# Layer two of a hybrid decoder trunk: half of K of both u blocks by seven products beside the V blocks

## The chip, the core and the metric

The kernel runs on one core of a Trainium2 chip. A core has a matrix engine (TensorE, PE in the profile, with its weight loads as PEld), a vector engine (VectorE, DVE), a scalar engine (ScalarE, ACT), a general one (GpSimd, POOL) and a queue that only issues transfers (SyncE, SP). Each engine works through its own instructions in order and waits on semaphores for the others. The metric is the device time of one execution in microseconds (us), lower is better.

## The reference

Two layers over x of 256 tokens by 2048 features, all in float32. What matters here is the first half of a layer:

```python
h = rms_norm(x, norm1_g[l])
z = h @ w_in[l]                       # columns: u 1024 | v 1024 | q 1024 | k 256 | v_attn 256
z_sgu = gelu(z[..., :2048])
u, v = split(z_sgu, 2)                # v: rms_norm per head of 64, then a causal 128x128 mix per head
out_a = u * (einsum('hts,bcshd->bcthd', tril(w_s), v) + b_s)
out_b = swa_sink_attention(q, k, v_attn)   # q and k normed per head, 16 query heads, window 128
mixed = concat(rms_norm(out_a), rms_norm(out_b))
x = x + mixed @ w_out[l]
x = x + (silu(h2 @ w_gate) * (h2 @ w_up)) @ w_down    # h2 = rms_norm(x, norm2_g), 5632 wide
```

## The kernel before

**A product in float32 from three matmuls.** Activations stand transposed in SBUF, 128 features by 256 tokens, as a pair of a high and a low part. Weights come as tiles of 128x1024 float32, two K-tiles of 512 columns (512 KB, `raw`, eight buffers). `split2` makes two tiles of each: ACT casts `wh` (five buffers), DVE subtracts for the rest `wl` (four buffers). `mm3` then issues high by high, high by low, low by high. A `unit` is one weight tile for both token halves, twelve matmuls of 128x512. PE, DVE and ACT thus go through the same list of weight tiles, DVE and ACT ahead by at most the buffers.

**Seven products.** A 2x2 block product (Strassen's scheme in Winograd's form) needs seven block products in place of eight. `seven` does it in five PSUM banks, `seven_low` in three. A step of these uses one weight tile for six matmuls (one combination of tokens), so each weight tile, split at the same cost, feeds half as many matmuls as in a unit. Sums of weight tiles are made by DVE (`raw` plus `ys`, `ss`) and by DMAs that accumulate, issued by POOL. The activations need sums as well, `ext`, which `combine` makes of the normed x. In both layers seven products serve q, gate and up (ten blocks of eleven), and half of K of two column blocks of `w_out`.

**The order of layer two's first half.** The code is emitted in the order of a clock (`tick`) that counts units. What hangs on a result is put off by so many units with `later` (numbers in tables such as `Q_T`, `SPATIAL_AT`, `U_AT`), and a scheduler then orders each engine's instructions. While the last down product of layer one runs, q of layer two goes beside it, thirty steps spread over `Q_UNITS` units by `q_to`. Blocks follow: k with v_attn, V0, V1, u0, u1, eight units each. The norms per head (`head_inv`) take squares on ACT, sums on DVE, a power on POOL (`inv_rms`, L210), and then a scaling on DVE (`scaled`, L583 for q in two pairs of halves, L732 for V). The six pieces of attention (`attend`) and the spatial mixes are strewn between the units of V1, u0 and u1. `u_gated` ends a u block. Then `PARTS` orders the units of `w_out` with the steps of its `seven_low` (`s`).

**PSUM.** Eight banks: five in `pa` (`acc`, `m`, `l`), two in `pd` (`dacc`), one in `pm`. Small tiles (scores, transposes) take turns in all three, or in `pm` alone while `solo` is set.

Of the kernel before, what the change touches and what calls it, by code (L numbers as in the profile page):

```python
# [12 lines left out]
F32 = mybir.dt.float32  # L13
# [36 lines left out]
UNIT_AT = ((7.5, 10, 12.5, 15.5, 18, 20.5), (8, 11, 14, 17, 21, 25))  # L50
KV_NORM = (31, 0)
KV_T = (8, 6)
# [8 lines left out]
Q_T = (((4, 6), (6, 9)), ((4, 6), (4, 7)))  # L61
SPATIAL_AT = (((8, 10), (9, 11)), ((6, 9), (7, 10)))
U_AT = (((5, 8), (2, 4)), ((3, 7), (2, 3)))
END_AT = (((21, 23.5), (25.9, 27)), ((22, 27), (31, 33)))
S_OUT = (True, True)
# [7 lines left out]
    "a0 a0 s a0 s a0 a1 a1 s a1 s a1 s b0 s b0 s b0 s b0 s b1 s b1 s b1 s b1 s s b2 b2 b2 b2 b3 b3 b3 b3",  # L73
# [14 lines left out]
def trunk(ctx, tc, x, xt, w_in, w_q, w_out, w_oa, w_gate, w_up, w_down, sgu_w, sgu_g, consts,  # L88
# [22 lines left out]

    def split2(raw):
        wh = wp.tile([P, 2, NB], F32R, tag="wh", name="wh", bufs=5)
        wl = wp.tile([P, 2, NB], F32R, tag="wl", name="wl", bufs=4)
        step = 2 if clock[0] > 1 else 1
        for j in range(0, 2, step):
            src = raw[:, j : j + step, :]
            nc.scalar.copy(wh[:, j : j + step, :], src)  # L118
            nc.vector.tensor_tensor(  # L119
                wl[:, j : j + step, :], src, f(wh[:, j : j + step, :]), ALU.subtract  # L120
            )
        return wh, wl
# [81 lines left out]
    anchor = [None]  # L204

# [91 lines left out]
    def combine(ps, lay, col, ext):  # L297
# [4 lines left out]
        extend(g, ap, "big", ext)  # L302
        return pair
# [96 lines left out]
    def seven_low(src, pairs, ext, out):  # L400
# [19 lines left out]
        def held(name):  # L420
            return tp.tile([P, 2, NB], F32, tag="hT", name=name)
# [3 lines left out]
        for i in range(2):  # L425
            x.append(raw_load(src(0, 0, i)))
            y.append(held("ys"))
            nc.sync.dma_start(y[i], src(0, 1, i))
            b22 = raw_load(src(1, 1, i))
            s.append(held("ss"))  # L430
            half(x[i], acc0, a_op(0, 0), i, True, True)
            yield
            nc.vector.tensor_tensor(x[i], x[i], y[i], ALU.add)
            nc.vector.tensor_tensor(s[i], x[i], b22, ALU.add)
            anchor[0] = nc.gpsimd.dma_start(y[i], src(1, 1, i), accum_op=ALU.add)
        acc1 = bank("l1")
# [15 lines left out]
        out(0, 0, acc0, 1)  # L452
# [3 lines left out]
        nc.vector.tensor_tensor(mp[:, 1], acc1, mp[:, 1], ALU.add)  # L456
        for i in range(2):
            half(s[i], acc2, a_op(1, 1), i, False, True)
            yield
            if i == 0:  # L460
                out(1, 1, mp[:, 1], -1)
        nc.vector.tensor_tensor(mp[:, 0], acc2, mp[:, 0], ALU.add)
        for i in range(2):
            half(raw_load(src(1, 1, i)), acc1, e_op(3), i, False, True)
            yield
            if i == 0:
                out(0, 1, mp[:, 0], 1)
        out(1, 0, acc1, -1)
# [42 lines left out]
    for lay in range(L):  # L511
# [62 lines left out]
        def q_norm(b, lay=lay, layer=layer, qT=qT, qz=qz):  # L574
# [10 lines left out]
            head_inv(qn, 8, scaled)  # L585
# [121 lines left out]
        def v_gate(b, acc, lay=lay, layer=layer, gate=gate, wms=wms):  # L707
# [69 lines left out]
        def norm_block(n, ss, pairs, lay, col, ext=None):  # L777
            def to_T(c):
                lo = n * NB + 2 * c * P
                ps = pm.tile([P, 2, SEQ], F32, tag="sm", name="ps_n")  # L780
                transpose_pair([xres[:, t, lo : lo + 2 * P] for t in range(NTOK)], ps)
                at = col + 4 * n + 2 * c
                pairs.append(
                    split_gain(ps, lay, at, "hT") if ext is None else combine(ps, lay, at, ext)
                )
# [22 lines left out]
        v_gate(0, run(block(2, *beside), with_q))  # L808
        if lay == 0:
            v_gate(1, run(block(3, *beside), with_q))  # L810
        if lay == 0:
# [5 lines left out]
        later(Q1_AT, lambda q_norm=q_norm: q_norm(1))  # L817
# [59 lines left out]
        def complete(n, whole=whole, ss2=ss2, pairs2=pairs2, ext2=ext2, norm_block=norm_block):  # L877
# [3 lines left out]

        low = seven_low(
            lambda r, c, i: w_oa[lay, c, i, r], pairs_a, ext_a,
            lambda c, t, acc, sign: residual(2 + c, t, acc, sign),
# [128 lines left out]
        def down(blocks, lay=lay, pairs_f=pairs_f, norm_block=norm_block, ss1=ss1, pairs1=pairs1, ext1=ext1, left=left, live=live, release=release, accs=accs, full=full, seed=seed, flush=flush, turn_over=turn_over):  # L1013
# [4 lines left out]
            def out_of(n, t, acc):  # L1018
# [12 lines left out]
                if t == NTOK - 1 and final and lay < L - 1:  # L1031
                    norm_block(n, ss1, pairs1, lay + 1, C_G1, ext1)
# [60 lines left out]
        for went in other:  # L1093
# [4 lines left out]
            if lay < L - 1 and done > 0:  # L1098
                q_to(now_q, done / Q_UNITS[1])

# [89 lines left out]
```

## Time and profile before

| | us |
|---|---|
| median of 3 runs (1913.45 to 1914.74) | 1914.46 |
| profiled execution, its time | 1913.7 |
| profiled execution, span from first to last instruction | 1912.0 |
| PE busy | 1903.6 |
| DVE busy | 1725.1 |
| ACT busy | 1361.0 |
| POOL busy | 183.4 |
| layer two, V1 to u1, in the span | about 1056 to 1133 |

PE's busy time is one of overlapping instructions, with modelled ends; the pace of matmuls is read from their starts in the timeline. "Idle before" gives how long an engine stood before an instruction and which instruction released it. Times in the span count from the first instruction.

### The profile page before, as it was taken

How to read it: one execution, taken by the hardware profiler on the slowest of the kernel's cores; microseconds unless marked ns; L12 is line 12 of the kernel's file. 1: busy time of each engine (PE TensorE's matmuls, PEld its weight loads, DVE VectorE, ACT ScalarE, POOL GpSimd, SP SyncE). 2: the span in 40 equal slices, each digit the busy share in tenths (PEclk: the TensorE clock that was granted, in tenths of full speed). 3: DMA queues.
4: the chain of work that ended last, by engine and by line, in shares of the span. 5: the costliest groups of instructions: out<-in, count | busy, mean ns of one | idle time of the engine just before them, and what ended most of it. 6: DMA issues, size and time to landing. Idle time of an engine off the chain costs nothing.

```text
span 1912.0 us, 25453 instructions
## 1 busy us (share of the span) xinstructions
PE 1903.6 (100%) x8764; PEld 1565.2 (82%) x8764; DVE 1725.1 (90%) x1879; ACT 1361.0 (71%) x1829; POOL 183.4 (10%) x180
## 2 busy tenths in 40 slices
PE   9999999999999999999999999999999999999999
PEld 7888888888888888888888888888888888888887
DVE  7988889999999999999797778899999999999993
ACT  8668676677767776777777576766867677776773
POOL 0230001000000001000012200000000100010000
PEclk9999999999999999999999999999999999999999
DMA  9874668878977897888577537697789788888783
GB/s 356 257 288 135 192 201 245 245 244 270 284 231 244 273 289 224 258 254 277 187 230 249 192 118 224 195 277 225 241 273 296 226 255 264 270 245 253 250 276 109
DMA packets 128289, 459.98 MB, mean 241 GB/s; under 512 B 14240, under 2 KB 14624, under 8 KB 128160
## 3 DMA queue, kind: packets, MB, share of 16 engines
q1 hardware_dynamic: 105552, 377.49, 53.7%
q0 software_dynamic: 21888, 79.70, 23.0%
q8 instruction: 68, 1.11, 0.2%
q10 hardware_dynamic: 720, 1.18, 0.2%
q14 instruction: 61, 0.50, 0.1%
HBM read 456.21 MB, written 2.10 MB: 240 GB/s over the span
## 4 chain that ended last, share of the span: by engine, by line
PE 95%; ACT 2%; issue 1%; DVE 1%; DMA 1%; POOL 0%; SPq 0%; DVEq 0%; ACTq 0%; POOLq 0%
PE m L155 15%; PE m L154 15%; PE m L156 15%; PE dacc L154 11%; PE dacc L155 11%; PE dacc L156 11%; PE acc L154 4%; PE acc L155 4%; PE acc L156 4%; PE ps_f L227 1%; PE ps_v L666 1%; PE l L154 1%; PE l L155 1%; PE l L156 1%; PE ps_n L227 1%
## 5 line engine op out<-in xcount | busy, mean ns | idle before, releaser
L118 ACT CAST wh<-raw 128x1024 fp32r<-128x1024 f32 (+1 forms) x794 | 814.7, 1050 | 384.5 <-DVE raw L350 168.3
L119 DVE TENSOR_TENSOR wl<-raw,wh 128x1024 fp32r<-128x1024 f32 (+1 forms) x794 | 945.1, 1219 | 92.4 <-ACT wh L118 26.5
L154 PE MATMUL m<-wh,ext 128*128 128x512 f32 x704 | 276.7, 393 | 0.0
L155 PE MATMUL m<-wl,ext 128*128 128x512 f32 x704 | 274.9, 391 | 0.0
L156 PE MATMUL m<-wh,ext 128*128 128x512 f32 x704 | 274.4, 390 | 0.0
L155 PE MATMUL dacc<-wl,aT 128*128 128x512 f32 x624 | 243.4, 390 | 0.0
L154 PE MATMUL dacc<-wh,aT 128*128 128x512 f32 x624 | 243.2, 391 | 0.0
L156 PE MATMUL dacc<-wh,aT 128*128 128x512 f32 x624 | 243.0, 389 | 0.0
L119 DVE TENSOR_TENSOR wl<-t,wh 128x1024 fp32r<-128x1024 f32 x176 | 213.6, 1223 | 12.9 <-issue 5.4
L118 ACT CAST wh<-t 128x1024 fp32r<-128x1024 f32 x176 | 184.4, 1051 | 37.3 <-DVE t L351 13.6
L154 PE MATMUL m<-wh,hT 128*128 128x512 f32 x528 | 206.4, 391 | 0.0
L155 PE MATMUL m<-wl,hT 128*128 128x512 f32 x528 | 205.7, 390 | 0.0
L156 PE MATMUL m<-wh,hT 128*128 128x512 f32 x528 | 205.5, 389 | 0.0
L155 PEld LDWEIGHTS m<-wl,ext 128*128 128x128 f32 x704 | 132.3, 188 | 28.9 <-DVE wl L119 2.0
L154 PEld LDWEIGHTS m<-wh,ext 128*128 128x128 f32 x704 | 132.2, 188 | 27.5 <-ACT wh L118 0.9
L156 PEld LDWEIGHTS m<-wh,ext 128*128 128x128 f32 x704 | 132.2, 188 | 27.4
L154 PEld LDWEIGHTS dacc<-wh,aT 128*128 128x128 f32 x624 | 117.1, 188 | 25.1 <-ACT wh L118 0.7
L155 PEld LDWEIGHTS dacc<-wl,aT 128*128 128x128 f32 x624 | 117.2, 188 | 24.8 <-DVE wl L119 0.6
L156 PEld LDWEIGHTS dacc<-wh,aT 128*128 128x128 f32 x624 | 117.2, 188 | 24.3
L359 POOL DMA_DIRECT2D t<-in_w_gate_dram x80 | 69.1, 864 | 525.9 <-DVE wl L119 389.7
L156 PEld LDWEIGHTS m<-wh,hT 128*128 128x128 f32 x528 | 99.1, 188 | 20.7
L155 PEld LDWEIGHTS m<-wl,hT 128*128 128x128 f32 x528 | 99.2, 188 | 20.3
(190 smaller groups left out, 2905.7 us busy)
## 6 DMA issues: line engine op xcount, KB each, us to landing
raw<-in_w_gate_dram SPq DMA_DIRECT2D x176, 512.0 KB, 6.1
raw<-in_w_up_dram SPq DMA_DIRECT2D x176, 512.0 KB, 6.0
raw<-in_w_down_dram SPq DMA_DIRECT2D x176, 512.0 KB, 6.0
t<-in_w_gate_dram POOLq DMA_DIRECT2D x80, 512.0 KB, 7.4
raw<-in_w_in_dram SPq DMA_DIRECT2D x76, 512.0 KB, 6.0
raw<-in_w_out_dram SPq DMA_DIRECT2D x48, 512.0 KB, 4.3
raw<-in_w_up_dram POOLq DMA_DIRECT2D x40, 512.0 KB, 6.1
raw<-in_w_q_dram SPq DMA_DIRECT2D x32, 512.0 KB, 4.9
```

The lines of the kernel that those rows point to most:

```text
L118: nc.scalar.copy(wh[:, j : j + step, :], src)
L119: nc.vector.tensor_tensor(wl[:, j : j + step, :], src, f(wh[:, j : j + step, :]), ALU.subtract)
L154: nc.tensor.matmul(acc, ah, wh, start=first, stop=False, skip_group_check=again)
L155: nc.tensor.matmul(acc, ah, wl, start=False, stop=False, skip_group_check=again)
L156: nc.tensor.matmul(acc, al, wh, start=False, stop=last, skip_group_check=again)
L227: nc.tensor.transpose(ps[:, j, t * P : (t + 1) * P], blocks[t][:, j * P : (j + 1) * P], ident)
L359: anchor[0] = nc.gpsimd.dma_start(t2, src(1, 0, i), accum_op=ALU.add)
L666: nc.tensor.matmul(pv[:, r, i], pt[:, (r * n + i) * (t + 1) + b, :], zkv[b][:, cols], start=b == 0, stop=b == t,)
```

## The change

Layer two's u blocks (1024 columns) are no longer sixteen units of `block(0)` and `block(1)`. For the first 1024 rows of K, `seven_low` makes the 2x2 block product (two column blocks by two token halves) in fourteen steps of six matmuls, beside eight units of V1 and the last four of V0; `U_ORDER` gives the order (`v` a unit of V, `s` a step), and the last four steps stand alone. Three results stand in the three banks of the scheme, the fourth (`c22`) in a bank of its own. Then eight units of the other half of K add to these four banks, and `u_gated` follows for both blocks. The scheme's sums of tokens are those that q of layer two already has (`ext1`), kept longer, so those of the first four pairs move to other buffers (`aT`). The weights come a second time in another arrangement (`w_uh`), made on the host.

V1 accumulates in `pa`, V0 in `pd` as before; after V0 the steps and V1 hold all five banks of `pa`.

Query: the thirty steps of q in layer two spread over 20 units in place of 24, with a power of 1.1 on their share. The scalings of q and of V in layer two are emitted with `issue_after` the last `wl`, and later by other gaps (`Q_GAP`, `V_GAP`). The tables for layer two are set anew. In `seven_low` the first sums of weights are emitted before the step's yield, and results go to four functions in `done`.

```diff
-Q_PACE = (1.5, 1)
-GAP = (4.5, 2.5)
+Q_PACE = (1.5, 1.1)
+GAP = (4.5, 4)
+V_GAP = ((4.5, 4.5), (6, 4))
...
-Q_UNITS = (20, 24)
-Q1_AT = 6
+Q_UNITS = (20, 20)
+Q1_AT = (6, 6)
+Q_GAP = (1.5, 2)
...
+U_ORDER = "v s v v s v v s v s v s v s v s v s v s v s"
...
-            nc.vector.tensor_tensor(
+            last_wl[0] = nc.vector.tensor_tensor(
                 wl[:, j : j + step, :], src, f(wh[:, j : j + step, :]), ALU.subtract
             )
...
+    def in_turn(then):
+        def held(r):
+            with tc.issue_after(last_wl[0].ins):
+                then(r)
+
+        return held
...
-    def seven_low(src, pairs, ext, out):
+    def seven_low(src, pairs, ext, done, tag="hT"):
...
-        out(0, 0, acc0, 1)
+        done[0, 0](acc0, None)
...
-        nc.vector.tensor_tensor(mp[:, 1], acc1, mp[:, 1], ALU.add)
+        done[1, 1](acc1, mp[:, 1])
...
-        nc.vector.tensor_tensor(mp[:, 0], acc2, mp[:, 0], ALU.add)
+        done[0, 1](acc2, mp[:, 0])
...
-        out(1, 0, acc1, -1)
+        done[1, 0](acc1, None)
...
-            head_inv(qn, 8, scaled)
+            head_inv(qn, 8, in_turn(scaled) if lay else scaled, Q_GAP[lay])
...
-                head_inv([v[:, t] for t in range(NTOK)], 8, scaled, GAP[lay])
+                head_inv([v[:, t] for t in range(NTOK)], 8, in_turn(scaled) if lay else scaled, V_GAP[lay][b])
...
         if lay > 0:
-            v_gate(1, run(block(3)))
-        for b in range(2):
-            u_gated(b, run(acc_u if lay == 0 and b == 0 else block(b)))
+            us = {}
+
+            def opposite(acc, z, us=us):
+                us[1, 1] = pa.tile([P, NB], F32, tag="acc", name="c22")
+                nc.vector.scalar_tensor_tensor(us[1, 1], acc, -1.0, z, ALU.mult, ALU.subtract)
+
+            def added(acc, z, us=us):
+                us[0, 1] = acc
+                nc.vector.tensor_tensor(acc, acc, z, ALU.add)
+
+            def turned(acc, z, us=us):
+                us[1, 0] = acc
+                nc.scalar.activation(acc, acc, AF.Copy, scale=-1.0)
+
+            low = seven_low(
+                lambda r, c, i: w_uh[0, c, i, r], pairs1, ext1,
+                {
+                    (0, 0): lambda acc, z, us=us: us.update({(0, 0): acc}),
+                    (1, 1): opposite, (0, 1): added, (1, 0): turned,
+                },
+                "aT",
+            )
...
+            v01 = itertools.chain(v_block(0, v0), v_block(1, block(3)))
+            n_v = 0
+            for name in U_ORDER.split():
+                if name == "s":
+                    next(low)
+                    continue
+                n_v += 1
+                next(v01, None)
+                solo[0] = n_v < 25 - Q_UNITS[1]
+                if n_v == 32 - Q_UNITS[1]:
+                    next(v01, None)
+            few[0] = False
+            for _ in range(4):
+                next(low)
+            next(low, None)
+            for b in range(2):
+                acc = [us[b, t] for t in range(NTOK)]
+                for c in range(4, 8):
+                    unit(
+                        w_in[lay, b, c], [(pairs1[c], 0), (pairs1[c], 1)], acc,
+                        False, c == 7, True,
+                    )
+                u_gated(b, acc)
...
-                q_to(now_q, done / Q_UNITS[1])
+                q_to(now_q, (done / Q_UNITS[1]) ** Q_PACE[1])
```

The engines' orders agree between the two kernels up to the end of layer one's last down product. Three places where they differ follow. The names: `wl` is the low part of a weight tile, `hT` and `ext` those of the normed x and its sums, `raw` and `t2` weight tiles and their sums, `ir` a norm's power, `wm` the spatial weights.

DVE, where q's steps go beside the last units of layer one's down product and k's first (the unit of `dacc` whose split is `wl_8952`, later `wl_8951`), before:

```order
L119 TENSOR_TENSOR wl_8952<-raw_8949,wh_8951 128x1024
L119 TENSOR_TENSOR wl_8975<-raw_8967,wh_8974 128x1024
L292 TENSOR_TENSOR ext_8906<-e_8869,ext_8906 128x512
L350 TENSOR_TENSOR raw_8967<-raw_8967,raw_8969 128x1024
L351 TENSOR_TENSOR t2_8973<-raw_8967,raw_8971 128x1024
L119 TENSOR_TENSOR wl_8987<-raw_8967,wh_8986 128x1024
L119 TENSOR_TENSOR wl_8999<-raw_8996,wh_8998 128x1024
L357 TENSOR_TENSOR raw_8969<-raw_8969,raw_8971 128x1024
L119 TENSOR_TENSOR wl_9016<-t2_8973,wh_9015 128x1024
```

And after:

```order
L124 TENSOR_TENSOR wl_8951<-raw_8948,wh_8950 128x1024
L313 TENSOR_TENSOR hT_8878<-g_8875,hT_8878 128x512
L294 SCALAR_TENSOR_TENSOR e_8881<-e_8881,g_8875 128x128
L304 TENSOR_TENSOR ext_8885<-e_8847,ext_8885 128x512
L297 SCALAR_TENSOR_TENSOR e_8881<-e_8881,g_8875 128x128
L362 TENSOR_TENSOR raw_8931<-raw_8931,raw_8933 128x1024
L304 TENSOR_TENSOR ext_8916<-e_8881,ext_8916 128x512
L363 TENSOR_TENSOR t2_8937<-raw_8931,raw_8935 128x1024
L124 TENSOR_TENSOR wl_8969<-raw_8931,wh_8968 128x1024
L369 TENSOR_TENSOR raw_8933<-raw_8933,raw_8935 128x1024
L124 TENSOR_TENSOR wl_8980<-t2_8937,wh_8979 128x1024
```

Before, four splits stood behind the first, three of steps and one of a unit; now there are two, both of steps, and the sums of x's last pair and of the weights stand in one piece ahead of them.

POOL from V0's spatial weights to the last norm of q and V, before:

```order
L695 DMA wm_9215<-in_sgu_w_dram 128x1024
L700 AFFINE_SELECT wm_9215<-wm_9215 128x1024
L604 DMA bias_9364<-in_band_dram 128x1024
L604 DMA bias_9366<-in_band_dram 128x1024
L210 TENSOR_TENSOR ir16_9394<-ms16_9392,mhalf_99 128x16
L210 TENSOR_TENSOR ir16_9423<-ms16_9421,mhalf_99 128x16
L695 DMA wm_9443<-in_sgu_w_dram 128x1024
L700 AFFINE_SELECT wm_9443<-wm_9443 128x1024
L210 TENSOR_TENSOR ir16_9554<-ms16_9552,mhalf_99 128x16
```

And after:

```order
L446 DMA ys_9306<-in_w_uh_dram 128x1024
L222 TENSOR_TENSOR ir16_9353<-ms16_9351,mhalf_99 128x16
L708 AFFINE_SELECT wm_9242<-wm_9242 128x1024
L446 DMA ys_9376<-in_w_uh_dram 128x1024
L452 DMA ss_9310<-in_w_uh_dram 128x1024
L452 DMA ss_9380<-in_w_uh_dram 128x1024
L222 TENSOR_TENSOR ir16_9460<-ms16_9458,mhalf_99 128x16
L703 DMA wm_9535<-in_sgu_w_dram 128x1024
L222 TENSOR_TENSOR ir16_9498<-ms16_9496,mhalf_99 128x16
```

The four accumulating DMAs of the u weights now stand in POOL's queue between the powers; `ir16_9460` is V0's and `ir16_9498` that of q's second pair.

ACT at the end of a u block's transposes, where the first units of `w_out` need `aT`, before (u0's second half, `ps_t_10177`):

```order
L309 ACTIVATE ge_10182<-ps_t_10177,cst_82 128x256 x2
L313 CAST aT_10185<-ge_10182 128x512
L753 ACT_TABLE_LOAD
L753 ACTIVATE u_10225<-acc0_9902,ir2_8791 128x512
L291 CAST ext_10209<-ge_10182 128x512
```

And after (u0's second half, `ps_t_10286`):

```order
L229 ACTIVATE aT_10274<-ps_t_10269,cst_82 128x256
L761 ACT_TABLE_LOAD
L761 ACTIVATE u_10300<-l1_9462,ir2_8808 128x512
L229 ACTIVATE aT_10274<-ps_t_10269,cst_82 128x256
L321 ACTIVATE ge_10291<-ps_t_10286,cst_82 128x256 x2
L761 ACTIVATE u_10302<-c22_9867,ir2_8808 128x512
L325 CAST aT_10294<-ge_10291 128x512
```

The table load and the two gelus of u1 have moved from behind the cast of u0's second half to ahead of it. On PE, that half's transposes stand before one unit and eight transposes ahead of the unit that reads it now (`w_10345`); before, two units, eight transposes and a piece's scores stood between (`w_10271`).

More of the change, by code (lines that the diff above doesn't have):

```diff
@@ L110, in raw_load @@
         return raw
+    last_wl = [None]
     def split2(raw):
@@ L420, in held @@
         def held(name):
-            return tp.tile([P, 2, NB], F32, tag="hT", name=name)
+            return tp.tile([P, 2, NB], F32, tag=tag, name=name)
         x, y, s = [], [], []
@@ L807, in trunk @@
         later(GATE_LOAD[lay][1], lambda gate_load=gate_load: gate_load(1))
-        v_gate(0, run(block(2, *beside), with_q))
         if lay == 0:
+            v_gate(0, run(block(2, *beside), with_q))
             v_gate(1, run(block(3, *beside), with_q))
+        else:
+            v0 = block(2, *beside)
+            for _ in range(Q_UNITS[1] - 16):
+                next(v0)
+                with_q()
         if lay == 0:
```

51 lines of the change are left out of this document (32 added, 19 removed).

## The prediction

> **What bounds the kernel.** First the page: its span, its busy times and the chain that ended last.
>
> ```profile
> span 1912.0 us, 25453 instructions
> ...
> PE 1903.6 (100%) x8764; PEld 1565.2 (82%) x8764; DVE 1725.1 (90%) x1879; ACT 1361.0 (71%) x1829; POOL 183.4 (10%) x180
> ...
> PE 95%; ACT 2%; issue 1%; DVE 1%; DMA 1%; POOL 0%; SPq 0%; DVEq 0%; ACTq 0%; POOLq 0%
> ```
>
> The chain is PE's. Next the waits, for PE over the whole span:
>
> ```profile
> PE heat L193 <- DVE mhalf L195: 1.5, 1, 1.5
> PE acc L154 <- ACT wh L118: 1.1, 1, 1.1
> PE ps_t L227 <- DVE s L622: 0.7, 1, 0.7
> PE acc L155 <- DVE wl L119: 0.2, 1, 0.2
> ```
>
> Four waits, 3.5 us. The kernel gets shorter only by fewer matmuls, or by small losses that are no whole waits. Their pace is read from PE's timeline in V1, the change's place (start, duration, then the instruction):
>
> ```profile
> 1056.05 0.48 PE L154 MATMUL acc<-wh,hT 128*128 128x512 f32 x1
> 1056.50 0.50 PE L155 MATMUL acc<-wl,hT 128*128 128x512 f32 x1
> 1056.84 0.40 PE L156 MATMUL acc<-wh,hT 128*128 128x512 f32 x1
> ...
> 1059.13 1.05 PE L718 MATMUL ps_g<-v,wm 128*128 128x128 f32 x8
> 1059.94 0.48 PE L154 MATMUL acc<-wh,hT 128*128 128x512 f32 x1
> ...
> 1060.71 0.39 PE L154 MATMUL acc<-wh,hT 128*128 128x512 f32 x1
> ...
> 1062.53 0.39 PE L156 MATMUL acc<-wh,hT 128*128 128x512 f32 x1
> 1062.76 0.27 PE L227 MATMUL ps_t<-ident,m 128*128 128x128 f32 x1
> ...
> 1063.11 0.48 PE L154 MATMUL acc<-wh,hT 128*128 128x512 f32 x1
> ...
> 1066.06 1.16 PE L617 MATMUL ps_s<-kT,qT 64*128 64x128 f32 x16
> 1067.15 0.50 PE L154 MATMUL acc<-wh,hT 128*128 128x512 f32 x1
> ```
>
> From 1060.71 to 1062.53 lie eight steps: 0.2275 us a matmul, 2.73 us a unit, 1.37 us a step of six. Four transposes take 0.35 (1062.76 to 1063.11), a spatial half 0.81 (from 1059.13), a piece's scores 1.09 (from 1066.06). At 1056 two matmuls took 0.45 and 0.34 us in place of 0.23 each: 0.33 us lost.
>
> What the others have left is in the windows. The columns after the window are its length, the busy time with the instructions of PE, PEld, DVE, ACT and POOL, then clock, DMA share and GB/s:
>
> ```profile
> 960.00:990.00 30.00, 30.00 (x140) 24.78 (x139) 29.31 (x43) 22.59 (x36) 5.61 (x3) 1.00 0.82 247
> ...
> 1050.00:1080.00 30.00, 29.89 (x159) 23.98 (x157) 23.65 (x37) 17.20 (x34) 12.45 (x5) 1.00 0.51 167
> 1080.00:1110.00 30.00, 30.00 (x179) 25.43 (x180) 23.21 (x38) 21.17 (x47) 1.12 (x2) 1.00 0.52 175
> 1110.00:1140.00 30.00, 30.00 (x168) 24.72 (x168) 21.09 (x37) 21.76 (x49) 0.00 (x0) 1.00 0.32 106
> ```
>
> From 1050 to 1140 DVE idles 22.1 us and ACT 29.9 us. From 960 to 990, where q begins, DVE idles 0.7 us.
>
> **The change part by part.** *Matmuls.* Eight units of twelve, 96 matmuls, become fourteen steps of six, 84. Twelve go, at 0.2275: -2.73 us. The Trainium skill, in TensorE: Matmul & The Clock Gate, section "Back-to-back issue gap", gives 131 ns as the sustained spacing at 512 columns. By it twelve would be worth 1.57 us and the sum below -0.60 (1913.9); this trace has 227.5 ns in all eight steps, so the rule gets no chance here.
>
> *DVE, ACT and transfers in bulk.* Prices from their timelines:
>
> ```profile
> 1049.85 0.69 DVE L732 TENSOR_TENSOR v<-v,ir 128x512 f32<-128x512 f32 x1 [1.64 <-POOL ir L210]
> ...
> 1054.02 0.69 DVE L583 TENSOR_TENSOR m<-m,ir 128x512 f32<-128x512 f32 x1 [1.58 <-POOL ir L210]
> 1054.63 0.69 DVE L583 TENSOR_TENSOR c<-c,ir 128x512 f32<-128x512 f32 x1
> 1055.23 2.35 DVE L119 TENSOR_TENSOR wl<-raw,wh 128x1024 fp32r<-128x1024 f32 x2
> 1057.50 1.27 DVE L252 TENSOR_REDUCE hs<-sq 128x8 f32<-128x512 f32 x2
> 1058.69 1.96 DVE L119 TENSOR_TENSOR wl<-raw,wh 128x1024 fp32r<-128x1024 f32 x1
> ```
>
> ```profile
> 1087.42 1.99 ACT L118 CAST wh<-raw 128x1024 fp32r<-128x1024 f32 x2
> ...
> 1100.31 1.28 ACT L753 ACT_TABLE_LOAD   x1
> 1101.61 1.27 ACT L753 ACTIVATE u<-acc,ir 128x512 f32<-128x512 f32 x2
> ...
> 1114.48 0.84 ACT L309 ACTIVATE ge<-ps_t,cst 128x256 f32<-128x256 f32 x2 [1.27 <-PE ps_t L227]
> ...
> 1115.82 0.62 ACT L313 CAST aT<-ge 128x512 fp32r<-128x512 f32 x1
> ```
>
> A split costs DVE 1.13 (two from 1055.23 to 1057.50), ops on 512 columns 0.6 (1054.02 to 1055.23 holds two). Six splits more, four sums of 128x1024 taken at a split's price and two of 512 make 12.5 us. ACT has six casts at 1.0, four copies or sign changes of 512 columns at 0.62 and one table load: 9.8 us. Both fit into 22.1 and 29.9, so in bulk this costs nothing; what hides it is that idle time, and without it all 12.5 us would come on top. Six transfers of 512 KB more meet a DMA share of 0.51, 0.52 and 0.32: nothing, as long as the weights arrive before the casts. Two raw buffers stay held for the scheme's first tiles and a third for its sums, so five of eight go round. Five units or steps, mixed, last about 10 us, and a transfer lands in 6.0:
>
> ```profile
> raw<-in_w_in_dram SPq DMA_DIRECT2D x76, 512.0 KB, 6.0
> ```
>
> *Scalings held behind splits.* Before, two scalings stood idle for a power with splits queued behind them, 1.64 and 1.58 us (the rows of 1049.85 and 1054.02). PE lost its 0.33 at 1056 right after. If that goes: -0.33, between 0 and -0.33.
>
> *The same wait, later.* POOL's timeline has what a power costs:
>
> ```profile
> 1045.91 3.90 POOL L210 TENSOR_TENSOR ir<-ms,mhalf 128x16 f32<-128x16 f32 x1 [20.54 <-DVE ms L208]
> 1050.70 3.29 POOL L210 TENSOR_TENSOR ir<-ms,mhalf 128x16 f32<-128x16 f32 x1 [0.89 <-DVE ms L208]
> 1053.94 0.60 POOL L695 DMA_DIRECT2D wm<-in_sgu_w_dram  x1
> ...
> 1149.27 0.92 POOL L435 DMA_DIRECT2D ys<-in_w_oa_dram  x1 [2.73 <-DVE rden L660]
> 1155.67 0.86 POOL L435 DMA_DIRECT2D ys<-in_w_oa_dram  x1 [5.48 <-ACT wh L118]
> ```
>
> Now V0's power, a weight transfer and the second pair's power follow each other: 3.9 + 0.6 + 3.9 = 8.4 us at most, 3.3 + 0.6 + 3.3 = 7.2 at least, from V0's sums of squares on. DVE meanwhile has two reductions (1.2) and two splits (2.27), then stands 3.7 to 4.9 us at the pair's scaling, with two scalings (1.2) and a split (1.13) to do after it: 6.0 to 7.2 us without a new split for PE. Its four `wl` buffers hold, at that place, a step, a unit, a step and the pieces between, 1.37 + 2.73 + 1.37 + 0.35 + 1.09 = 6.9 us of PE's work. I take +0.3, the excess of the longer powers, since 3.9 stands beside 3.29; ends 0 and +1.5, a step's length.
>
> *Query denser.* Between the splits `wl_8951` and `wl_8980` DVE's order now has three sums of weights (3.4), two splits (2.27) and three ops of 512 columns (1.8), 7.5 us with two short ones left out. PE needs the last of them after a unit and a step, 4.1 us. Before, between `wl_8952` and `wl_9016`, four splits, three sums and one op, 8.5 us, stood against two units and two steps, 8.2. DVE must be 3.4 us ahead there where 0.3 did. It was not held by full buffers from 960 to 990, since it hardly idled, so how far ahead it is can't be read. Ends 0 and +3.4; I take +0.5, near the lower end, since the nearest row (960 to 990) shows DVE busy for 29.31 us beside a PE that never stops.
>
> *Transposes of u0 before the cast.* Behind u0's second transposes ACT now has half a copy of `aT` ahead (0.42), the table load (1.28), a gelu (0.64), 0.42, two `ge` (0.84), a gelu (0.64) and the cast (0.62): 4.9 us, and DVE's subtraction 0.6, in all 5.5. PE has a spatial half, four transposes, a unit and eight transposes, 0.81 + 0.35 + 2.73 + 0.70 = 4.6, and two matmuls that need the cast alone, 0.45. Short by 0.45 to 0.9: I take +0.5, ends 0 and +0.9. For this table load the Trainium skill, in ScalarE: Activation LUTs, section "What ACT_TABLE_LOAD costs", gives 1.28 us and a drain of 1.38 with every switch. By it the term would be +1.9 and the sum -0.4 (1914.1); here the gelu starts at 1101.61, 0.02 after the load's end, so the drain is not seen and gets no chance.
>
> *V1's gelu between steps.* Table load, two gelus and two squares, 1.28 + 1.27 + 1.26 = 3.8, and a cast and split, 2.1, against four steps and their pieces from V1's end on (5.5 for the steps alone, 0.81, 1.09 and 0.70 for spatial half, scores and transposes, 8.1 in all): 0, and up to +1.5 if ACT comes there behind by the exponentials of a piece. The sum of the third bank on DVE stands behind two score ops (1.8 us), with the same lead of 2 us: 0.
>
> *`w_out`'s new order* moves no work: 0, between -0.5 and +0.5.
>
> The sum: -2.73 - 0.33 + 0.3 + 0.5 + 0.5 = -1.76 us. The profiled execution took 1913.7, 0.76 below the median; I carry the difference to the median: 1914.46 - 1.76 = 1912.7.
>
> **The rivals.** *Covered throughout.* All waits stay inside the buffers: -2.73 - 0.33 = -3.06, 1911.4. For it speaks that PE waited 3.5 us in all; against it the three thin margins.
>
> *q's start uncovered.* DVE has no lead where q is denser: +3.4 in place of +0.5, 1915.6. For it speaks DVE's 29.31 of 30; against it that PE never waited there.
>
> *Powers behind accumulating transfers (slower).* In POOL's queue V0's power stands behind the four new transfers. Each issue waits until ACT and DVE have read the tile. In `w_out` such issues were late by 2.73 and 5.48 us (rows above). As the cover is spent, each microsecond of lateness is one of PE. From 1.8 us on the gain is gone; at 5.48 the sum is +3.7, 1918.2; with both, 8.2 us, +6.4, 1920.9. It is slower by more than 0.2% from 5.6 us on. Against it: in DVE's order both reads stand ahead of the sums of squares.
>
> *The bulk does not fit.* This would need the idle 22.1 us at the wrong places; it is the last rival's case with another name, and has no chance of its own.
>
> **How the numbers follow.** A measurement of this kernel tells about 0.2%, 3.8 us, from no change. The forecast has 0.48, covered throughout 0.22, q's start 0.12, POOL's queue 0.18. Faster by more than 0.2% needs -3.8; covered throughout gives -3.06, and 0.7 more of the pace's small losses would have to go, so 0.08 of its 0.22. Slower by more comes from POOL's queue, 0.15, and a twelfth of the rest, 0.05. Same: 0.72. The range goes from 1910.8 (covered, with `w_out`'s -0.5) to 1918.2 (POOL's queue with one wait).
>
> **What would show it.** PE should have 8752 matmuls, and PE's waits between 1040 and 1140 should stay below 1.5 us. The profile would show the wait at the pair's scaling as DVE's for `ir`, with PE waiting for `wl` after it, and the wait at u0 as PE's for `aT` or a matmul of `w_out` that starts late. Wrong if PE waits over 5 us in that stretch, or if the stretch from k's block to `w_out` shortens by over 3.5.

## The result, and the profile after

| | before | changed |
|---|---|---|
| median of 20 runs each, side by side, us | 1914.08 (1913.16 to 1914.93) | 1910.74 (1909.64 to 1912.57) |
| ratio | | 0.9983, 95% interval 0.9976 to 0.9990 |
| span of the profiled execution, us | 1912.0 | 1907.9 |

The gain is 3.3 us (interval 1.9 to 4.6): below the 0.2% that was called "same", but clear of zero. The forecast was 1.8 us. The profiled execution of the changed kernel was the fastest of its 20, so the two spans differ by 4.1. First the page of the changed kernel and PE's waits over the whole span:

```profile
span 1907.9 us, 25455 instructions
...
PE 1899.6 (100%) x8752; PEld 1562.5 (82%) x8752; DVE 1736.6 (91%) x1891; ACT 1369.6 (72%) x1840; POOL 183.9 (10%) x184
```

```profile
PE heat L198 <- DVE mhalf L200: 1.5, 1, 1.5
PE acc L159 <- ACT wh L123: 0.9, 1, 0.9
PE ps_t L239 <- DVE s L630: 0.7, 1, 0.7
```

DVE gained 11.5 us of work, ACT 8.6, and PE lost 12 matmuls; the waits fell from 3.5 to 3.1 us. No wait is listed for PE between 900 and 1200. The windows that answer to those of before:

```profile
960.00:990.00 30.00, 30.00 (x142) 24.70 (x141) 29.33 (x43) 22.46 (x36) 3.27 (x3) 1.00 0.84 263
1050.00:1080.00 30.00, 30.00 (x166) 24.05 (x165) 25.50 (x35) 22.88 (x47) 7.32 (x6) 1.00 0.65 206
1080.00:1110.00 30.00, 30.00 (x183) 25.34 (x183) 25.36 (x40) 24.01 (x52) 4.30 (x2) 1.00 0.64 208
1110.00:1140.00 30.00, 30.00 (x177) 25.52 (x177) 21.06 (x43) 24.86 (x54) 0.00 (x0) 1.00 0.28 91
```

From 1050 to 1140 DVE still idles 18.1 us and ACT 18.3.

**Where the gain lies.** Two marks on PE stand at the same work in both kernels: the start of a unit of layer one's last down product, and the first matmul of layer two's gate, behind `w_out`. Of before, then of the changed kernel:

```profile
911.32 0.48 PE L154 MATMUL dacc<-wh,aT 128*128 128x512 f32 x1
...
1229.65 0.39 PE L154 MATMUL dacc<-wh,hT 128*128 128x512 f32 x1
```

```profile
911.05 0.47 PE L159 MATMUL dacc<-wh,aT 128*128 128x512 f32 x1
...
1225.52 0.39 PE L159 MATMUL dacc<-wh,hT 128*128 128x512 f32 x1
```

(V1's matmuls begin at 1042.09 in before, where `acc` follows `dacc`, and not at about 1056; those of `w_out` begin at 1133.65.) 318.33 us became 314.47: 3.86 of the 4.1 us by which these two spans differ. Added up from each matmul's start to the next one's, the large matmuls give 3.35 of it (2.73 for twelve at 0.2275, and 0.62 net of small losses: the 0.33 at 1056 went, 0.25 came where query is denser, the rest is spread over many places) and the small ones (scores, transposes, mixes) 0.52. The largest single item among the small ones is a group that had not been priced: in before, eight transposes waited for ACT to finish the exponentials one by one, and the scores right behind them for the `qT` that ACT made next (it ended at 1078.79).

```profile
1076.83 1.67 PE L654 MATMUL ps_p<-ident,s 128*128 128x128 f32 x8
1078.43 1.54 PE L617 MATMUL ps_s<-kT,qT 64*128 64x256 f32 x8
```

The reason stands in DVE's queue. The scores of that piece were there from 1066.06 on, but the bias was added at 1070.56, behind the splits that had waited with the second pair's scaling (`ir`, 2.82 us from 1061.9), and ACT stood for the maximum that follows:

```profile
1064.68 1.29 DVE L583 TENSOR_TENSOR c<-c,ir 128x512 f32<-128x512 f32 x2 [2.82 <-POOL ir L210]
...
1070.56 1.28 DVE L622 SCALAR_TENSOR_TENSOR s<-ps_s,bias 128x512 f32<-128x512 f32 x2
```

```profile
1074.92 0.40 ACT L638 ACTIVATE s<-s,nm 128x128 f32<-128x128 f32 x1 [2.37 <-DVE nm L632]
```

In the changed kernel scores, bias and transposes of that piece are:

```profile
1057.93 1.16 PE L625 MATMUL ps_s<-kT,qT 64*128 64x128 f32 x16
...
1069.08 1.03 PE L662 MATMUL ps_p<-ident,s 128*128 128x128 f32 x8
```

```profile
1059.12 1.29 DVE L630 SCALAR_TENSOR_TENSOR s<-ps_s,bias 128x512 f32<-128x512 f32 x2 [0.42 <-PE ps_s L625]
```

The bias is added 1.2 us behind the scores in place of 4.5, and the eight transposes take 0.79 us from start to next start in place of 1.60.

**The three margins of the forecast.** From the changed kernel's timelines: DVE at the pair's scaling, POOL's two powers ahead of it, and PE's next unit:

```profile
1055.14 1.29 DVE L591 TENSOR_TENSOR c<-c,ir 128x512 f32<-128x512 f32 x2 [2.82 <-POOL ir L222]
1056.35 1.22 DVE L124 TENSOR_TENSOR wl<-raw,wh 128x1024 fp32r<-128x1024 f32 x1
```

```profile
1047.91 2.93 POOL L222 TENSOR_TENSOR ir<-ms,mhalf 128x16 f32<-128x16 f32 x1 [0.86 <-DVE ms L220]
1050.81 0.62 POOL L703 DMA_DIRECT2D wm<-in_sgu_w_dram  x1
1051.45 3.66 POOL L222 TENSOR_TENSOR ir<-ms,mhalf 128x16 f32<-128x16 f32 x1
```

```profile
1059.02 0.50 PE L159 MATMUL acc<-wh,hT 128*128 128x512 f32 x1
1059.36 0.39 PE L160 MATMUL acc<-wl,hT 128*128 128x512 f32 x1
```

DVE stood 2.82 us; the split behind it ended at 1057.6, and PE used it at 1059.36. So 1.8 us of lead were left. DVE had made no split for 5.3 us (2.82, two scalings in 1.2, and the split's 1.2). At query's denser start and behind u0's second transposes nothing was left, and next to nothing was lost (PE's timeline at both places, then ACT's):

```profile
993.55 0.39 PE L159 MATMUL m<-wh,ext 128*128 128x512 f32 x1
993.91 0.50 PE L160 MATMUL m<-wl,ext 128*128 128x512 f32 x1
994.25 0.40 PE L161 MATMUL m<-wh,ext 128*128 128x512 f32 x1
...
1136.88 0.50 PE L159 MATMUL acc<-wh,aT 128*128 128x512 f32 x1
```

```profile
1136.19 0.64 ACT L325 CAST aT<-ge 128x512 fp32r<-128x512 f32 x1
```

Two matmuls at 993.6 took 0.36 and 0.34 in place of 0.23 (0.25 us lost); the cast ended at 1136.83, 0.05 us ahead of the matmul behind it.

### The profile page after: what moved, and what is told of

Same layout as the page of the kernel before. It is cut to its first block, busy times and chain, and to the rows that moved or that the text cites. A ratio compares the mean times of both kernels' runs of the same rounds, so it can differ in the third digit from the quotient of the medians.

```text
span 1907.9 us, 25455 instructions
## 1 busy us (share of the span) xinstructions
PE 1899.6 (100%) x8752; PEld 1562.5 (82%) x8752; DVE 1736.6 (91%) x1891; ACT 1369.6 (72%) x1840; POOL 183.9 (10%) x184
## 4 chain that ended last, share of the span: by engine, by line
PE 96%; ACT 1%; issue 1%; DVE 1%; DMA 0%; POOL 0%; SPq 0%; DVEq 0%; ACTq 0%; POOLq 0%
PE m L160 15%; PE m L159 15%; PE m L161 15%; PE dacc L159 11%; PE dacc L160 11%; PE dacc L161 11%; PE acc L160 4%; PE acc L159 4%; PE acc L161 4%; PE l L159 1%; PE l L161 1%; PE l L160 1%; PE ps_f L239 1%; PE ps_v L674 1%; PE ps_n L239 1%
## 5 line engine op out<-in xcount | busy, mean ns | idle before, releaser
L123 ACT CAST wh<-raw 128x1024 fp32r<-128x1024 f32 (+1 forms) x794 | 814.2, 1050 | 364.7 <-DVE raw L362 168.8
L161 PEld LDWEIGHTS m<-wh,hT 128*128 128x128 f32 x528 | 99.1, 188 | 20.6
L159 PEld LDWEIGHTS m<-wh,hT 128*128 128x128 f32 x528 | 99.1, 188 | 20.3
```

Source lines behind the costliest of these rows:

```text
L159: nc.tensor.matmul(acc, ah, wh, start=first, stop=False, skip_group_check=again)
L161: nc.tensor.matmul(acc, al, wh, start=False, stop=last, skip_group_check=again)
```

## The experiments

All were timed beside the kernel before, 11 executions each (7 of e10_q_sooner, 8 of e13_both). "Against before" is the difference of the medians; the changed kernel stands at -3.3. "Between the marks" is the change of the stretch between the two marks above in the profiled execution; the changed kernel stands at -3.86. It is one execution of each, but free of what varies at the start of a run: the traces reach the first mark between 911.0 and 913.5 us. Behind the second mark the traces are alike within about 0.4 us.

| run | median, us | against before | ratio, 95% interval | between the marks |
|---|---|---|---|---|
| e1_pieces | 1916.97 | +2.7 | 1.0014, 1.0005 to 1.0022 | +2.44 |
| e2_in_turn | 1914.21 | 0.0 | 1.0000, 0.9991 to 1.0009 | -0.36 |
| e3_twelve | 1914.53 | +0.3 | 1.0002, 0.9993 to 1.0011 | +0.45 |
| e4_free | 1911.06 | -3.2 | 0.9986, 0.9977 to 0.9995 | -3.28 |
| e10_q_sooner | 1920.68 | +6.9 | 1.0031, 1.0020 to 1.0043 | +5.88 |
| e11_q_24 | 1916.57 | +2.8 | 1.0012, 1.0003 to 1.0021 | +2.02 |
| e12_twelve_u | 1912.73 | -1.1 | 0.9993, 0.9985 to 1.0002 | -1.00 |
| e13_both | 1918.98 | +5.2 | 1.0026, 1.0016 to 1.0037 | +4.56 |
| e7_power1 | 1912.86 | -1.3 | 0.9991, 0.9983 to 1.0000 | -1.90 |
| e7_power2 | 1917.16 | +3.0 | 1.0015, 1.0006 to 1.0023 | +2.88 |
| e9_loads | 1912.79 | -1.4 | 0.9991, 0.9982 to 1.0000 | -0.90 |
| e6_pace | 1910.87 | -3.3 | 0.9982, 0.9973 to 0.9990 | -3.15 |

### Is a matmul worth its pitch?

The first term of the sum, taken alone: twelve matmuls fewer, nothing else.

```diff
+                if short[0] and j == 0 and t == 1:   # twelve times from V1 on
+                    ...                              # high by high, high by low; low by high left out
+                    continue
                 mm3(
```

> The kernel before with twelve matmuls fewer: in V1's eight units and u0's first four, the product of the low part of the activations with the high part of the weights is left out for one K-tile and one token half each. All transfers, casts and splits stay. Theory A: 12 x 0.2275 = 2.73 us less. Rival B (the sustained spacing of 131 ns that the Trainium skill states is what a matmul is worth): 1.57 us less. Rival C (DVE is what sets that stretch): under 1 us less, with PE waits for wl in place of the rest.

Nothing was gained. PE only reached the same places sooner and waited there:

```profile
1055.58 0.47 PE L154 MATMUL acc<-wh,hT 128*128 128x512 f32 x1
1056.41 0.50 PE L155 MATMUL acc<-wl,hT 128*128 128x512 f32 x1 [0.36 <-DVE wl L119]
...
1075.45 2.78 PE L662 MATMUL ps_p<-ident,s 128*128 128x128 f32 x8
...
1152.37 0.40 PE L154 MATMUL acc<-wh,aT 128*128 128x512 f32 x1
1153.25 0.50 PE L156 MATMUL l<-wh,aT 128*128 128x512 f32 x1 [0.48 <-DVE aT L322]
```

At 1055.58 PE stood 0.83 us from one start to the next (0.23 is the pitch) for a split behind the two scalings, and at 1152.37 0.88 us for a transposed pair that DVE had not finished. The largest item lies between: the transposes of exponentials that stalled in before took 2.71 us to the next start, from 1075.45, in place of 1.60. Rival C's size holds, its reason only in part, since DVE's splits set one of the three places: matmuls taken away there only bring PE sooner to what it waits for. PE's 3.5 us of listed waits had said nothing of that: at these places the other engines stood just ahead.

The same twelve in u0 and u1, where DVE idles more:

```diff
-            short[0] = 12
             v_gate(1, run(block(3)))
+            short[0] = 12
         for b in range(2):
```

> The kernel before with twelve matmuls fewer as in the last such run, but left out in u0's eight units and u1's first four (again the low part of the activations by the high part of the weights for one K-tile and one token half in each). Theory A (a matmul is worth 0.2275 us where DVE is ahead; in V1 it was not, in u0 and u1 it is): 2.2 to 2.8 us less than before. Rival B (DVE or ACT bounds the whole stretch): under 1 us less, as in V1.

1.1 us less, with an interval that reaches from 2.9 less to 0.4 more: by the time alone neither theory is shut out. Between the marks it is 1.0 less, at the edge of rival B and far from theory A. The trace shows what took part of it back. Three of the shortened units of u0 lie ahead of the piece that stalled; its transposes began 0.63 us sooner than before, at 1076.20, the exponentials did not, and the group took 2.46 us to the next start in place of 1.60. At 1151.04 PE stood 0.87 us for the same pair as in the run before:

```profile
1076.20 2.54 PE L662 MATMUL ps_p<-ident,s 128*128 128x128 f32 x8
...
1151.04 0.39 PE L154 MATMUL acc<-wh,aT 128*128 128x512 f32 x1
1151.91 0.50 PE L156 MATMUL l<-wh,aT 128*128 128x512 f32 x1 [0.48 <-DVE aT L322]
```

0.9 and 0.6 us of the 2.73 go back at these two places alone. So it isn't only V1: where a piece or a transposed pair is finished just ahead of PE, as at these two places, the time of matmuls taken out ahead of it is lost again.

### What gave the cover back?

Query as before, with the seven products:

```diff
-Q_UNITS = (20, 20)
+Q_UNITS = (20, 24)
-U_ORDER = "v s v v s v v s v s v s v s v s v s v s v s"
+U_ORDER = "v s v s s v s v s s v s v s v s v s"
```

> The changed kernel with query over 24 units as before; the ten steps of the scheme that stood beside V0's end and V1 then stand beside V1's eight units alone. Theory A (the seven products pay only because the query pair's scalings are out of V1; without it the splits stand behind waits for a power while steps need a split every 1.37 us): 2 us or more slower than the changed kernel, PE waits for wl, time about that of before. Rival B (the twelve matmuls count by themselves): within 0.8 us of the changed kernel.

2.8 us slower than before, 6.1 slower than the changed kernel (2.0 and 5.9 between the marks). Theory A, and more than its 2 us; but the other tables stay those that were set for the earlier end, and what share of the loss is theirs no run shows. Its DVE and POOL, and PE behind them:

```profile
1056.56 0.69 DVE L591 TENSOR_TENSOR m<-m,ir 128x512 f32<-128x512 f32 x1 [3.29 <-POOL ir L222]
```

```profile
1049.58 6.95 POOL L222 TENSOR_TENSOR ir<-ms,mhalf 128x16 f32<-128x16 f32 x2
```

```profile
1059.04 0.50 PE L160 MATMUL l<-wl,ext 128*128 128x512 f32 x1 [2.11 <-DVE wl L124]
...
1061.10 0.63 PE L161 MATMUL acc<-wh,hT 128*128 128x512 f32 x1
```

V0's power and the first pair's follow each other (6.95 us), DVE stands for them, and PE waits 2.11 us for a split. It then ran seven matmuls at a pitch of 0.427 us.

Is query's earlier end enough by itself? On the kernel before, without and with the twelve matmuls left out:

```diff
-Q_UNITS = (20, 24)
+Q_UNITS = (20, 20)
...
+            v0 = block(2, *beside)
+            for _ in range(4):
+                next(v0)
+                with_q()
...
+            v_gate(0, run(v0))
             v_gate(1, run(block(3)))
```

> The kernel before with query of layer two over 20 units in place of 24 and its norms and attention counted from V0's fourth unit (the pieces' and ends' times four units later in the table, so that they keep their places); no seven products, no holding of scalings. Theory A (the three waits of DVE for a power, 1.64, 1.58 and 2.82 us between 1048 and 1065, all fell into V1; now two of them fall into V0): the lost 0.33 us at 1056 goes, and the time is 0.3 us below before, with nothing lost at query's denser start or up to 0.25. Rival B (what is taken from V1 is lost where query is denser): 0.5 us or more above before.

> Query four units sooner and twelve matmuls fewer in V1 and u0's first half (the same products left out), on the kernel before. Theory A (query's earlier end gives V1 its cover back): 2.5 to 3.2 us less than before, where the twelve alone gave nothing. Rival B (V0's own wait for its power, 1.64 us, with splits behind it is enough to eat them): under 1.5 us less.

Both theories failed in both runs: these are 6.9 and 5.2 us slower. Only the first run's rival B had expected a loss, and that where query is denser. The first pair's scaling, whose power came at 1053, was itself late for PE's transposes. It also took 1.58 us in place of 0.69, beside POOL's mask of `wm` (from 1053.04 for 1.09 us; see the last section). Of the run without the twelve left out: DVE, PE, and the window behind the wait, where the clock's column is 0.54:

```profile
1053.09 1.58 DVE L583 TENSOR_TENSOR m<-m,ir 128x512 f32<-128x512 f32 x1 [3.05 <-POOL ir L210]
```

```profile
1054.72 0.33 PE L227 MATMUL ps_t<-ident,m 128*128 128x128 f32 x1 [3.76 <-DVE m L583]
```

```profile
1055.50:1059.20 3.70, 3.70 (x14) 2.94 (x13) 2.88 (x5) 1.73 (x3) 1.44 (x1) 0.54 0.15 46
```

These transposes are set by the old times (`Q_T` 4 and 6, or 4 and 7, units behind the norm); the changed kernel has 5 and 7, or 5 and 8, and other gaps. So the earlier end alone, with the old times, is a loss. The changed kernel has its cover from the end, the times and the order of steps together; which of them gives how much, no run here parts. The twelve matmuls are worth 1.7 us between these two runs (1.3 between the marks). That doesn't show that query's end made room for them: in these two runs PE stands 3.8 and 3.5 us in V1's first half, and such a wait gives DVE and ACT a lead for what follows too.

### The scalings held behind splits

```diff
-head_inv(..., in_turn(scaled) if lay else scaled, V_GAP[lay][b])
+head_inv(..., scaled, V_GAP[lay][b])
```

(and the same for query, with `Q_GAP`.)

> The changed kernel with the scalings of layer two no longer held behind the splits; the order on DVE alone differs. V0's first scaling then stands right behind the sums of squares, about 2.9 us before its power is there, with two splits behind it that came at 1049.9 in the changed kernel. Theory A (DVE is 1.8 to 2.8 us ahead of PE there, and that is enough): 0 to 0.3 us slower than the changed kernel, a few matmuls late around 1054. Rival B (the hold is what lets the change fit): 1.5 us or more slower, with PE waiting for wl.

3.2 us less than before, against 3.3. Rival B falls. Where theory A had put it PE lost 0.64 us, twice what it allowed (0.76 and 0.34 us from start to start, the last of four transposes ends the row ahead):

```profile
1054.27 0.48 PE L159 MATMUL acc<-wh,hT 128*128 128x512 f32 x1
1055.03 0.50 PE L160 MATMUL acc<-wl,hT 128*128 128x512 f32 x1 [0.28 <-DVE wl L124]
```

On the kernel before, the hold alone, with the changed gaps (for query in the same way, with its gap at 2):

```diff
-head_inv([v[:, t] for t in range(NTOK)], 8, scaled, GAP[lay])
+head_inv([v[:, t] for t in range(NTOK)], 8, in_turn(scaled) if lay else scaled, ((4.5, 4.5), (6, 4))[lay][b])
```

> The kernel before with the scalings of q and V in layer two held behind the last split of weights, with the changed kernel's gaps, and nothing else. Theory A: the two matmuls that took 0.45 and 0.34 us at 1056 take 0.23 again, 0.33 us less. Rival B: the scaling comes later and meets the next power, the wait stays with other names, no change within 0.1 us in that stretch. Either is far below what the median of five rounds can show, so the stretch in the trace decides.

(V0's first spatial half keeps its old time, so it reads V before its scaling here; the values differ, the work does not.) The pair of late matmuls at 1056 is gone, as theory A said, and DVE's waits for a power are longer, 2.71 and 3.89 us in place of 1.58 and 2.82. The median did not move, and between the marks the trace is 0.36 us shorter. So the hold is worth a few tenths, as the forecast's -0.33 said, and it isn't what lets the change fit.

### The piece that stalled

```diff
-UNIT_AT = (..., (8, 11, 14, 17, 21, 25))
+UNIT_AT = (..., (9.5, 12, 14.5, 17.5, 21, 25))
```

> The kernel before with the changed kernel's times for the six pieces of attention in layer two, and nothing else. Theory A (part of the gain is a piece that no longer stalls: before, eight transposes of exponentials from 1076.83 took 1.60 us and the scores behind them 1.47, against 0.79 and 1.06 where nothing is late): those two groups fall back, the time is 0.8 to 1.2 us below before. Rival B (what stalls there is the place in the row of units, whatever piece comes): the stall shows at another place, 0 +- 0.4 us.

2.7 us slower. The stall grew: in PE's timeline of this run the eight transposes took 2.52 us from 1086.54 to the next start.

```profile
1086.54 2.68 PE L654 MATMUL ps_p<-ident,s 128*128 128x128 f32 x8
```

Theory A falls: the new times by themselves cost. Rival B has the place right, but not the size (0 +- 0.4). In this run the bias was added 7.4 us behind the scores (1081.86 against 1074.43): in DVE's queue it now stands behind V1's scaling, which waited 3.08 us for its power and began at 1078.31. So the stall hangs on what stands ahead of the bias in DVE's queue; the table only moves the piece along it. In the changed kernel the bias follows its scores closely.

### How much cover is left at the pair's scaling

```diff
-        anchor[0] = nc.gpsimd.tensor_tensor(r, ms, mhalf[:, :n], ALU.pow)
+        for _ in range(1 + slow[0]):      # slow: 1 or 2 for V0 in layer two
+            anchor[0] = nc.gpsimd.tensor_tensor(r, ms, mhalf[:, :n], ALU.pow)
```

> The changed kernel with V0's power computed twice on POOL, one after the other; the order of all engines is else the same. In the changed kernel the two powers took 2.93 and 3.66 us, DVE stood 2.82 us for the second pair's, and the split behind it ended 1.8 us before PE's second matmul of the next unit used it (1057.6 against 1059.4). Theory A (DVE's lead there is all the cover that is left): 2.9 to 3.7 us more on POOL, less 1.8: 1.1 to 1.9 us slower than the changed kernel, PE waiting for wl around 1060. Rival B (the lead is made up by full buffers elsewhere): under 0.4 us slower.

> As the run with V0's power computed twice, now three times. Theory A (past the lead each microsecond of POOL is one of PE): 5.8 to 7.4 less 1.8, 4.0 to 5.6 us slower than the changed kernel. Theory C (a wait of 2.5 us or more also sets the matmuls behind it to a pitch of 0.427 us for some 3.4 us, as the runs with query moved showed): 1.4 to 1.6 us more than that, 5.4 to 7.2 slower, and the granted clock near 0.5 in that stretch. Rival B: under 0.8 us slower.

Against before -1.3 and +3.0, so 2.0 and 6.3 us slower than the changed kernel (2.0 and 6.7 between the marks). The first is theory A, at the upper end of its range, and the place is the one it named (DVE's timeline of that run, then PE's):

```profile
1057.74 1.29 DVE L596 TENSOR_TENSOR c<-c,ir 128x512 f32<-128x512 f32 x2 [5.17 <-POOL ir L225]
1058.95 2.12 DVE L124 TENSOR_TENSOR wl<-raw,wh 128x1024 fp32r<-128x1024 f32 x1
```

```profile
1061.12 0.50 PE L160 MATMUL acc<-wl,hT 128*128 128x512 f32 x1 [1.34 <-DVE wl L124]
```

The scaling came 2.6 us later (1057.74 against 1055.14), the split behind it took 0.9 longer, and 3.5 less 1.8 of lead is 1.7; PE's step took 1.85 us there in place of 0.34, 1.5 more. The second is theory C: past the lead a microsecond of POOL is one of PE, and the matmuls behind a long wait are slower as well. PE waited 4.32 us up to 1064.29, and then nine matmuls stood 0.427 us apart:

```profile
1064.29 0.79 PE L160 MATMUL acc<-wl,hT 128*128 128x512 f32 x1 [4.32 <-DVE wl L124]
...
1068.29 0.63 PE L160 MATMUL acc<-wl,hT 128*128 128x512 f32 x1
```

### The table load ahead of u0's cast, and query's pace

```diff
                 nc.scalar.activation(u, acc[t], AF.Gelu, scale=layer["rstd1"][t])
+                if lay == 1 and b == 1 and t == 0:
+                    nc.scalar.activation(tab[:, 0:1], u[:, 0:1], AF.Exp)
```

> The changed kernel with an exponential of one column of u1's first half between its two gelus, so that ACT loads its tables twice more: one load (1.28 us) and a short activation come right ahead of the cast of u0's second pair, one load behind it. In the changed kernel that cast ended at about 1136.8 and the matmul that reads it began at 1136.88. Theory A (there is next to no margin): PE is 1.2 to 1.5 us late there, 1.0 to 1.6 us slower in all. Rival B (PE takes other matmuls of w_out first, so that the cast is covered): under 0.4 us.

1.9 us slower than the changed kernel by the medians, 3.0 between the marks, so theory A's size was low, and its place was wrong. The scheduler put other matmuls of `w_out` ahead of those that read the late cast (from 1138.55 in this trace), as rival B said, but its size (under 0.4) was wrong as well. The time was then lost later: ACT had 2.8 us more to do (two loads of 1.28 and the exponential), and the casts and splits behind it came late, with 0.34, 0.57 and 0.99 us of waits from 1150 to 1161. The last:

```profile
1160.89 0.50 PE L160 MATMUL acc<-wl,aT 128*128 128x512 f32 x1 [0.99 <-DVE wl L124]
```

```diff
-Q_PACE = (1.5, 1.1)
+Q_PACE = (1.5, 1.3)
```

> The changed kernel with the power on query's share at 1.3 in place of 1.1: fewer steps in its first units, more in its last. Theory A (in the changed kernel DVE's lead was down to 0.05 us at 993.9, and two matmuls there took 0.36 and 0.34 us): these two fall back to 0.23, 0.2 us less in that stretch, nothing else. Rival B (the steps saved at the start are late at the end, and the second pair's norms with them): 0.5 us or more slower than the changed kernel, with waits around 1030 to 1060.

No change against the changed kernel by the medians; between the marks 0.7 us are lost. The two late matmuls at 993.6 went, and a larger loss came, neither theory's: 0.87 us passed from the matmul of 981.30 to a transposition of the norm, in place of 0.23. Why ACT was later there isn't shown.

```profile
982.17 0.66 PE L239 MATMUL ps_n<-ident,xres 128*128 128x128 f32 x4 [0.47 <-ACT g L283]
```

No run was faster than the changed kernel.

## Why the prediction was right or wrong

*Size.* 1912.7 was forecast from a base of 1914.46; on the base measured beside it the forecast's -1.76 is 1912.3, and 1910.74 came, a hair below the range's lower end (1910.8) as written, and inside it once the range moves with the base (1910.4). The direction, and that it stays within 0.2%, were right. The case that came is the rival "covered throughout" (-3.06), to which 0.22 was given and to the likeliest 0.48. Between the marks the gain is 0.8 more than that rival's, 0.5 of it from small groups that the sum did not hold.

*The three thin margins* (+0.3, +0.5, +0.5) are the terms that were mis-sized; together they came to about 0.25. At the pair's scaling DVE stood 2.82 us where 3.7 to 4.9 were reckoned: the powers took 7.2 us with the transfer between them, the forecast's least, and DVE spent part of that on a wait for ACT (0.54 us) ahead of its two splits, which wasn't reckoned. So 5.3 us passed without a new split in place of 6.0 to 7.2, while the cover was as reckoned: 5.3 and the 1.8 left are 7.1, against 6.9. That these 1.8 us were there to spare is shown by the run with one power more. Query's start cost 0.25, with the lead used up to the last tenth. At u0's cast ACT's half copy and half a table load were already done when the transposes ended, since PE came to them through a spatial half; of the 0.45 to 0.9 reckoned next to nothing came, with 0.05 us to spare.

*The matmuls* (-2.73). As a sum this held: the large matmuls give 3.35 in the two traces, 0.62 of it small losses. As a reason it was incomplete. It was taken for granted that twelve matmuls less are 2.73 us less, and the "idle 22.1 us" of DVE was called the cover. Left out by themselves in V1 and half of u0 they gave nothing. In the changed kernel they count because query's end, the times and the steps were moved together: with query's end as before and the rest kept, the seven products are 2.8 us slower than before. The forecast priced these moves as costs alone. That the number came near in spite of it is luck in part.

*The figure beside it, 131 ns a matmul.* The pitch in the changed kernel is 0.2275 us still (1056.48 to 1057.61, five matmuls). The Trainium skill, in TensorE: Matmul & The Clock Gate, section "Back-to-back issue gap", gives 131 ns as the sustained spacing; the measured pitch shuts that out here. The time alone would not: with the margins at nothing the sum by that figure is -1.9, the edge of the measured interval.

*The scalings held* (-0.33): a few tenths, as said; 0.64 us at that place in the trace without the hold, 0.2 in the medians, and 0.36 between the marks with the hold alone.

*Powers behind accumulating transfers* (0.18): didn't come; the last of these transfers was issued at 1046.19, ahead of V0's sums of squares. The price that it was given, each microsecond of lateness one of PE once the cover is spent, held for the wait of 1.34 us and was too low for those of 2.11 us and more.

*Not in the sum at all:* the piece that stalled at 1076.83, 0.8 us on its transposes and 0.4 on the scores behind them, less what the changed kernel loses at other small groups (0.52 in all). It stood in the profile of before, in the length of one group.

*What would show it.* 8752 matmuls, and no PE wait over 1.5 us from 1040 to 1140: right. The wait for `ir` at the pair's scaling: there, but without PE's wait for `wl` behind it. "From k's block to `w_out`" was a bad ruler, since steps and pieces cross both of its ends: from k's first matmul to the first of `w_out` it shortened by 1.3 us (161.0 to 159.7), below the 3.5 of the sign, while 28 small matmuls more stand in it. Over the marks above it is 3.86.

## What to carry to other kernels

Where PE is 100% busy with few waits, that doesn't make each of its instructions worth its pitch: take a dozen out at the place in question and measure, before a restructuring is priced by their number. A cover is best measured by lengthening the work that it hides, a step at a time; here that gave about 1.8 us where the order alone gave bounds from 0 to 1.5. And the length of each kind of small group should be compared over all its instances: one that takes twice as long as its like is a wait that the list of waits doesn't name.

## What the runs showed that was not expected

*Longer waits on PE cost more than themselves.* A wait of 1.34 us left the pitch at 0.2275. After waits of 2.11, 3.5 (the run with both), 3.76 and 4.32 us the matmuls ran at a pitch of 0.427 us; the granted clock was 0.53, 0.54 and 0.50 in the stretches behind the first, third and fourth. After 2.11 and 3.76 us this lasted some 3.4 us and cost about 1.6 more, and it began only 1.3 and 0.9 us after PE had gone on (1060.3 after 1059.0, 1055.6 after 1054.7). After 4.32 us the clock was already down in the wait (0.76 on the mean from 1060 to 1064), ten matmuls took 4.4 us, and the extra is 2.1 us, more than the 1.4 to 1.6 of theory C. Between 1.34 and 2.11 us nothing was measured. The Trainium skill, in TensorE: Matmul & The Clock Gate, section "HAM oscillation — how this bites in real kernels", speaks of idle gaps over some 3.4 us; here one of 2.1 was enough, so the measurement decides.

*DVE beside POOL's mask.* In the changed kernel a sum of 128x1024 took 2.12 us in place of 1.22, while POOL masked `wm`:

```profile
1036.82 2.12 DVE L445 TENSOR_TENSOR ss<-raw 128x1024 f32<-128x1024 f32 x1
```

```profile
1036.05 1.81 POOL L708 TENSOR_SCALAR_AFFINE_SELECT wm<-wm 128x1024 f32<-128x1024 f32 x1
```

POOL ended at 1037.86, and the sum 1.08 later, about its own time alone. The split of 2.12 us in the run with one power more (from 1058.95) ends 1.08 us behind POOL's mask too (from 1058.61 for 1.38). The Trainium skill, in SBUF — State Buffer, section "Who interferes with whom", says that a DVE instruction with two SBUF inputs contends with a GpSimd instruction that reads SBUF; these rows agree. It is 0.9 us on the engine whose lead was 1.8, and in that run it fell on the split that PE was waiting for.
